# The down projection of a gated MLP as seven products of halves instead of eight

## The chip, the cores and the metric

The kernel runs on one core of a Trainium2 chip. The metric is the device time of one execution in microseconds. TensorE (PE) does the matmuls, VectorE (DVE) and ScalarE (ACT) the elementwise work, GpSimd (POOL) some of it; SyncE (SP) issues nearly all transfers between DRAM and the on-chip memory SBUF. Matmul results land in PSUM, which has eight banks of 128x512 fp32 values.

## The reference, cut to what matters

The layer takes 512 tokens of width 1024. Two attention branches are mixed by gates and added to the residual; then comes the MLP that is changed here, and a last gated addition that uses the same residual:

```python
h = rmsnorm(x, mlp_pre_norm[i])
u = causal_dwconv(h @ w_up[i], conv_w[i], conv_b[i])
u_gate, u_val = jnp.split(u, 2, axis=-1)
ff = (jax.nn.gelu(u_gate, approximate=True) * u_val) @ w_down[i]   # (512 x 2816) @ (2816 x 1024)
x = x + rmsnorm(ff, mlp_post_norm[i])
e = p[i] @ w_ple[i]
x = x + jax.nn.sigmoid(rmsnorm(x, ple_norm[i]) @ w_ple_gate[i]) * e
```

## The kernel before, in words

Every fp32 operand of a matmul is kept as two tiles of a rounded format, `hi` and `lo`, with hi + lo close to the value. `split` (L71) makes them: ACT copies the source to `hi` (L72), DVE subtracts it from the source to get `lo` (L73). `mm3` (L75) then does three matmuls (hi times hi, hi times lo, lo times hi) for every product of a 128x128 stationary tile with a 128x512 moving tile. All matmuls carry line 56, the helper that issues them.

`chunk` (L137) streams weights: SP loads 128x1024 fp32 values (512 KB) into a `raw` tile, and `split` writes a `hi` and a `lo` tile. From the output projection on, these come from rings (`wtile`, L123): 3 raw tiles, 4 hi tiles and 4 lo tiles. A tile of a ring is written again only when the last reader of its earlier use is through.

The up projection runs over 22 pairs j of 128 gate and 128 value columns (L803). A pair needs 48 matmuls of 128x512 (`up_mms`) with `hT`, the normalized tokens, as moving operand, in two PSUM banks; four pairs of banks take turns. `conv_gelu` (L764) follows: for each of the two halves one ACT and two DVE instructions of 128x512 (the convolution), then the gelu on ACT, one multiplication on DVE, and a `split` of the 128x512 result into `ffh[j]` and `ffl[j]`. These 22 tiles live in `xp` (j to 7), `qkp` (j to 15) and `fp` (the last six).

The down projection (`down_pass`, L819) multiplies 512 tokens (four blocks n of 128), 2816 rows (22 tiles k) and 1024 columns (two halves of 512). It goes over the first column half for all four blocks, then over the second for blocks 0 and 1, then again over the second for blocks 2 and 3, 11 weight chunks each time; all eight PSUM banks hold `yd[n][half]`. `post_norm` (L708) normalizes a block, adds it to the residual `xn` and normalizes again; `to_hT` (L725) transposes the result on PE. Blocks 0 and 1 are normalized beside the pass over blocks 2 and 3; blocks 2 and 3 beside the gate matmuls of blocks 0 and 1 (`gate_mms`, L851).

The order of instructions on each engine is not written out by hand. A planner lists them: on each engine, among those that its model of time has ready, it takes the first of the program, or one marked by `hot`. The order is then fixed: each engine and SP's queue works its list from front to back, and an instruction that waits holds all behind it.

Of the kernel before, what the change touches and what calls it, by code (L numbers as in the profile page):

```python
# [8 lines left out]
F32 = mybir.dt.float32  # L9
# [3 lines left out]
ALU = mybir.AluOpType  # L13
# [24 lines left out]
def hybrid_kernel(ctx, tc, T):  # L38
# [634 lines left out]
    for f in (close_ca, close_wk, close_gap, close_sp, close_cqp, close_kvp, close_yp):  # L673
# [128 lines left out]
    g_post, g_next = loadgain(T["mlp_post"]), loadgain(T["ple_norm"])  # L802
    for j in range(2, NPAIR):  # L803
        if j in (8, 16):
            if j == 16:
                fp, close_fp = opened(name="fp", bufs=1, side="right")
            for l, t in ((ffh, "kT"), (ffl, "qT")):
                w = min(8, NPAIR - j)
                f = (qkp if j == 8 else fp).tile([P, w, S], F32R, name="ff" + t, tag=t)
                l.extend(f[:, i, :] for i in range(w))  # L810
# [6 lines left out]
    yd = [banks(n, "yd") for n in range(NB)]  # L817

    def down_pass(half, blocks):  # L819
        for c in range(NPAIR // 2):  # L820
            hi, lo = chunk(T["wd"][half * (NPAIR // 2) + c])
            for kk in range(2):
                k = 2 * c + kk
                w = slice(kk * S, (kk + 1) * S)
                for n in blocks:
                    b = slice(n * P, (n + 1) * P)
                    mm3(yd[n][half], ffh[k][:, b], ffl[k][:, b], hi[:, w], lo[:, w], k == 0, k == NPAIR - 1)

    down_pass(0, range(NB))
    down_pass(1, (0, 1))  # L830
    ts = {n: post_norm(n, yd[n], g_post, g_next) for n in (0, 1)}
    down_pass(1, (2, 3))
    ts[2] = post_norm(2, yd[2], g_post, g_next)
    for n in (0, 1):
        to_hT(n, ts[n])
    ts[3] = post_norm(3, yd[3], g_post, g_next)
    for n in (2, 3):
        to_hT(n, ts[n])


    close_fp()
# [18 lines left out]
    def last_halves(n, half):  # L860
        g = [bank(n, "pg") for _ in range(2)]
        b = slice(n * P, (n + 1) * P)
        for i in range(2):
            u = slice(half * S + i * 256, half * S + (i + 1) * 256)
            for k in range(8):
                hi, lo = cg[k]
                mm3(g[i][:, :256], hT[0][:, k, b], hT[1][:, k, b], hi[:, u], lo[:, u], k == 0, k == 7)
            o = lp.tile([P, S], F32, name="o", tag="o", bufs=4)[:, :256]
            act.activation(o, g[i][:, :256], AF.Sigmoid)
            dve.tensor_tensor(o, o, e[:, n, u], ALU.mult)  # L870
            dve.tensor_tensor(o, o, xn[:, n, u], ALU.add)
# [12 lines left out]

    pg = {(n, half): bank(n, "pg") for n in (0, 1) for half in range(2)}
    gate_mms(pg, (0, 1), (0, 1))
    raw = lp.tile([P, 1024], F32, name="wraw", tag="wraw", bufs=2)
    nc.sync.dma_start(raw, T["pT"].rearrange("p a b -> p (a b)"))
    split(ph.rearrange("p a b -> p (a b)"), pl.rearrange("p a b -> p (a b)"), raw)
    for k in range(2):  # L890
        raw = lp.tile([P, 1024], F32, name="wraw", tag="wraw", bufs=2)
        nc.sync.dma_start(raw, T["wp"][k])
        split(wph[:, k, :], wpl[:, k, :], raw)
    for n in range(NB):
# [15 lines left out]
            gate_mms(g, (n,), (half,))  # L910
            finish(n, half, g[n, half])

    for f in (close_lp, close_ck, close_xnp, close_bcp, close_rawb, close_qkp, close_rawp, close_psp,
              close_hp, close_wb, close_wa, close_xp, close_cpool):
        f()


def layouts(i):
# [16 lines left out]
    wd = np.asarray(i["w_down"])[0].reshape(NPAIR // 2, 2, P, 2, 512).transpose(3, 0, 2, 1, 4)  # L935
    col = lambda v: np.asarray(v).reshape(-1, P).T
    cw = np.asarray(i["conv_w"])[0].reshape(3, 2, NPAIR, P).transpose(0, 3, 2, 1).reshape(3, P, 2 * NPAIR)
    cb = np.asarray(i["conv_b"])[0].reshape(2, NPAIR, P).transpose(2, 1, 0).reshape(P, 2 * NPAIR)
# [21 lines left out]
        "wd": f(wd.reshape(NPAIR, P, 1024)),  # L960
# [45 lines left out]
```

## Time and profile before

| | |
|---|---|
| median of 3 runs | 751.62 us (751.62 to 752.12) |
| the profiled execution | 753.03 us, its span 751.3 us |
| PE busy | 739.1 us, 98% of the span, 3562 matmuls and transposes |
| DVE, ACT, POOL busy | 468.8 us (62%), 349.3 us (46%), 55.5 us (7%) |
| granted TensorE clock, mean | 0.999 of full speed |
| DMA | 81.29 MB, 108 GB/s mean |

The span is the time from the first to the last instruction; what lies around it is the difference to the execution's own time. A matmul's row shows its latency; the next one starts before it ends, so the cost of one is the distance between starts.

### The profile page before, as it was taken

The page shows a single profiled execution, that of the slowest core. Times are in us where ns is not written, and L with a number is a line of the kernel's source. Part 1 is how long each engine was busy: PE and PEld are TensorE (multiplying, and loading weights), DVE is VectorE, ACT ScalarE, POOL GpSimd, SP SyncE. Part 2 cuts the span into 40 slices and gives each one's busy share as a digit, 9 for nine tenths or more (in the row PEclk, how much of TensorE's full clock was granted, in tenths as well). Part 3 has the DMA queues.
Part 4 walks back from the last instruction along what each step waited for, and adds up shares of the span by engine and source line. Part 5 has one row for each costly group of instructions (what it writes and reads, how often), then busy time and mean ns, then how long its engine had stood idle before and what let it go on. Part 6 is the DMA issues. An engine that isn't in the chain of part 4 may idle for free.

```text
span 751.3 us, 9409 instructions
## 1 busy us (share of the span) xinstructions
PE 739.1 (98%) x3562; PEld 615.2 (82%) x3562; DVE 468.8 (62%) x817; ACT 349.3 (46%) x610; POOL 55.5 (7%) x46
## 2 busy tenths in 40 slices
PE   8999999999999999999999999999999999999997
PEld 8988877778888868899888888888888888888886
DVE  6567788986786394757565655666563213486742
ACT  5743577845453243637444444443433114355621
POOL 0104023100000070200000000000000000011200
PEclk9999999999999999999999999999999999999999
DMA  8611221122121327234323232323233233566211
GB/s 300 238 51 64 61 78 49 57 65 76 57 77 65 135 91 282 79 114 117 108 85 111 85 112 85 110 87 95 101 90 106 85 107 127 187 187 215 76 56 57
DMA packets 25582, 81.29 MB, mean 108 GB/s; under 512 B 3296, under 2 KB 4576, under 8 KB 25536
## 3 DMA queue, kind: packets, MB, share of 16 engines
q1 hardware_dynamic: 25536, 80.68, 32.7%
q8 instruction: 28, 0.46, 0.2%
q14 instruction: 18, 0.15, 0.1%
HBM read 78.11 MB, written 2.10 MB: 107 GB/s over the span
## 4 chain that ended last, share of the span: by engine, by line
PE 91%; DVE 7%; issue 1%; DMA 1%; ACT 0%; SPq 0%; DVEq 0%
PE pu L56 29%; PE yd L56 16%; PE psg L56 11%; PE pg L56 6%; PE yo L56 5%; PE puh L56 3%; PE psA L56 3%; PE psba L56 3%; PE psC L56 2%; PE psB L56 2%; PE scm L56 2%; PE pe L56 1%; PE pb L56 1%; PE pvm L56 1%; DVE wlo L73 1%; PE ptm L60 1%
## 5 line engine op out<-in xcount | busy, mean ns | idle before, releaser
L73 DVE TENSOR_TENSOR wlo<-wraw,whi 128x1024 fp32r<-128x1024 f32 (+2 forms) x114 | 140.2, 1231 | 142.6 <-ACT whi L72 139.2
L72 ACT ACTIVATE whi<-wraw 128x1024 fp32r<-128x1024 f32 (+4 forms) x120 | 123.2, 1026 | 159.9 <-PE yd L56 67.1
L56 PE MATMUL pu<-hT,whi 128*128 128x512 f32 x640 | 197.0, 389 | 0.0
L56 PEld LDWEIGHTS pu<-hT,whi 128*128 128x128 f32 x640 | 120.1, 188 | 25.0
L56 PE MATMUL pu<-hT,wlo 128*128 128x512 f32 x320 | 124.5, 389 | 0.0
L56 PEld LDWEIGHTS pu<-hT,wlo 128*128 128x128 f32 x320 | 60.1, 188 | 12.3
L56 PE MATMUL psg<-xh,whi 128*128 128x512 f32 x128 | 51.1, 399 | 1.3 <-DVE ga L422 0.9
L56 PE MATMUL psg<-xl,whi 128*128 128x512 f32 x128 | 50.8, 397 | 0.0
L56 PE MATMUL psg<-xh,wlo 128*128 128x512 f32 x128 | 50.8, 397 | 0.0
L56 PE MATMUL yd<-whi,ffqT 128*128 128x512 f32 x112 | 44.5, 397 | 0.0
L56 PE MATMUL yd<-wlo,ffkT 128*128 128x512 f32 x112 | 44.4, 396 | 0.0
L56 PE MATMUL yd<-whi,ffkT 128*128 128x512 f32 x112 | 44.1, 396 | 0.0
L775 ACT ACTIVATE cv<-cv 128x512 f32<-128x512 f32 x22 | 13.9, 633 | 43.6 <-DVE cv L774 43.6
L715 POOL TENSOR_TENSOR q<-q,mhalf 128x1 f32<-128x1 f32 x8 | 5.3, 657 | 376.8 <-DVE q L714 376.5
L774 DVE SCALAR_TENSOR_TENSOR cv<-pu,pp,cv 128x510 f32<-128x510 f32 x40 | 29.9, 749 | 1.4
L772 ACT ACTIVATE cv<-pu,pp 128x512 f32<-128x512 f32 x40 | 30.5, 761 | 0.0
L56 PEld LDWEIGHTS psg<-xh,whi 128*128 128x128 f32 x128 | 24.1, 188 | 7.0 <-DVE ga L422 1.1
L773 DVE SCALAR_TENSOR_TENSOR cv<-pu,pp,cv 128x511 f32<-128x511 f32 x40 | 29.8, 744 | 0.0
L56 PEld LDWEIGHTS psg<-xl,whi 128*128 128x128 f32 x128 | 24.1, 188 | 4.9 <-issue 0.2
L56 PEld LDWEIGHTS psg<-xh,wlo 128*128 128x128 f32 x128 | 24.1, 188 | 4.8
L72 ACT ACTIVATE ffkT<-cv 128x512 fp32r<-128x512 f32 x14 | 8.9, 633 | 39.1 <-DVE cv L776 39.1
L56 PEld LDWEIGHTS yd<-wlo,ffkT 128*128 128x128 f32 x112 | 21.1, 188 | 5.1
(264 smaller groups left out, 1482.5 us busy)
## 6 DMA issues: line engine op xcount, KB each, us to landing
wraw<-in_wup SPq DMA_DIRECT2D x44, 512.0 KB, 3.4
wraw<-in_wd SPq DMA_DIRECT2D x33, 512.0 KB, 3.4
wraw<-in_wg SPq DMA_DIRECT2D x16, 512.0 KB, 3.4
wraw<-in_wo SPq DMA_DIRECT2D x8, 512.0 KB, 4.2
wraw<-in_wpg SPq DMA_DIRECT2D x8, 512.0 KB, 3.5
xnat<-in_x SPq DMA_DIRECT2D x4, 512.0 KB, 6.4
wraw<-in_wba SPq DMA_DIRECT2D x4, 512.0 KB, 3.4
wraw<-in_wbb SPq DMA_DIRECT2D x4, 512.0 KB, 3.4
```

The lines of the kernel that those rows point to most:

```text
L56: pe.chain(out, nc.tensor.matmul(out, *a, **k))
L60: pe.chain(out, nc.tensor.transpose(out, *a))
L72: act.activation(hi, src, AF.Copy)
L73: dve.tensor_tensor(lo, src, f32(hi), ALU.subtract)
L715: pool.tensor_tensor(r1, v, mhalf[:, :1], ALU.pow)
L772: act.activation(c, u, AF.Identity, scale=w2, bias=cb)
L773: dve.scalar_tensor_tensor(c[:, 1:], u[:, :S - 1], w1, c[:, 1:], ALU.mult, ALU.add)
L774: dve.scalar_tensor_tensor(c[:, 2:], u[:, :S - 2], w0, c[:, 2:], ALU.mult, ALU.add)
L775: act.activation(cs[0], cs[0], AF.Gelu_apprx_tanh)
```

## The change

The result of the down projection is cut into four quarters: token halves 1 and 2 (256 each) by column halves 1 and 2. With A the activations, cut into token halves and two sets of rows (even and odd tiles of 128: pairs c = 0 to 10), and B the weights, cut likewise, the four quarters come from seven products M1 to M7 of sums of A's quarters with sums of B's quarters, each of 256 tokens by 1408 rows by 512 columns.

The sums of A are formed while the up projection runs, once per two pairs j (`ff_sums`): four of the seven operands are split into `FF` in SBUF, three are split and written to DRAM (`d1`, `d2`). The residual `xn` is written to DRAM (`xd`) after the attention part and its SBUF space serves for the sums (`X`); it is loaded again later. The down projection then runs in three stages. Stage 1, over c: M1, M5, M7 and M6 in all eight banks; the weight sums T1, T3 (`t13`) and T2 are formed on DVE. Stage 2, after `drain` has taken the banks' contents: M2 on top of M1, and M3; operands `p1` come back from DRAM, and the odd weight rows are loaded and split a second time. Stage 3: M4, with `p2` from DRAM. Blocks 0 and 1 are normalized beside stage 3, blocks 2 and 3 after it.

```diff
     def post_norm(n, ps, gp, gn):
+        xn = res["xn"]
...
             ts[n] = post_norm(n, yo[n], g_post, g_next)
+            nc.sync.dma_start(xd[n], res["xn"][:, n, :])
...
+    def ff_sums(c):
+        X = Xs.pop(c)
+        dve.tensor_tensor(X[:, 1], X[:, 7], X[:, 6], ALU.add)
+        dve.tensor_tensor(X[:, 3], X[:, 0], X[:, 7], ALU.subtract)
+        dve.tensor_tensor(X[:, 2], X[:, 1], X[:, 0], ALU.subtract)
+        dve.tensor_tensor(X[:, 5], X[:, 4], X[:, 2], ALU.subtract)
+        split(*ff_home(c), X[:, 0:4])
+        h = qp.tile([P, 3, 256], F32R, name="f2h", tag="f2h", bufs=2)
+        l = X[:, 4:7].bitcast(F32R)
+        act.activation(h, X[:, 4:7], AF.Copy)
+        dve.tensor_tensor(l, X[:, 4:7], f32(h), ALU.subtract)
+        for i, v in enumerate((h, l)):
+            nc.sync.dma_start(d1[c][:, i], f32(v[:, 0:2]))
+            nc.sync.dma_start(d2[c][:, i], f32(v[:, 2]))
...
-        dve.tensor_tensor(cs[0], cs[0], cs[1], ALU.mult)
-        split(ffh[j], ffl[j], cs[0])
+        dve.tensor_tensor(Xs[c][:, 4:7:2] if odd else Xs[c][:, 0:8:7], halves(cs[0]), halves(cs[1]), ALU.mult)
+        if odd:
+            ff_sums(c)
...
+    T2t = [hp.tile([P, 8, S], F32, name=f"T2{i}", tag=f"hT{i}") for i in range(2)]
+    T2 = [T2t[c // 8][:, c % 8] for c in range(NC)]
+    T13 = [T2t[1][:, 4 + 2 * i:6 + 2 * i].rearrange("p a t -> p (a t)") for i in range(2)]
+    order4 = ("M1", "M5", "M7", "M6")
...
+    for c in range(NC):
+        r1, r2 = wtile("raw", F32), wtile("raw", F32)
+        nc.sync.dma_start(r1, T["wd"][2 * c])
+        nc.sync.dma_start(r2[:, :S], T["wd"][2 * c + 1][:, B2])
+        t13 = T13[c % 2]
+        h1, l1, h2, l2 = (wtile(k, F32R) for k in ("hi", "lo", "hi", "lo"))
+        split(h1[:, B1], l1[:, B1], r1[:, B1])
+        dve.tensor_tensor(t13[:, B1], r1[:, B2], r1[:, B1], ALU.subtract)
+        dve.tensor_tensor(t13[:, B2], r2[:, :S], r1[:, B2], ALU.subtract)
+        dve.tensor_tensor(T2[c], r2[:, :S], t13[:, B1], ALU.subtract)
+        split(h2, l2, t13)
+        split(h1[:, B2], l1[:, B2], T2[c])
...
+        for m, s in zip(order4, (0, 1, 3, 2)):
+            mms(M[m], [t[:, s] for t in FF[c]], rhs[m], c == 0, c == NC - 1)
+
+    g_post, g_next = loadgain(T["mlp_post"]), loadgain(T["ple_norm"])
+    for n in range(NB):
+        nc.sync.dma_start(xn[:, n, :], xd[n])
...
+    hot(drain)
...
+        nc.sync.dma_start(f32(p1[c]), d1[c])
...
+    for c in range(NC):
+        raw = wtile("raw", F32)
+        nc.sync.dma_start(raw, T["wd"][2 * c + 1])
+        h, l = wtile("hi", F32R), wtile("lo", F32R)
+        split(h, l, raw)
+        dve.tensor_tensor(T4[c], raw[:, B1], T2[c], ALU.subtract)
...
+    for n in range(2):
+        dve.tensor_tensor(V12[n], M3[n], V12[n], ALU.add)
+        ts[n] = post_norm(n, (M["M1"][n], V12[n]), g_post, g_next)
...
+        split(h[:, w], l[:, w], T4[c])
+        mms(M4, [p2[c][:, i] for i in range(2)], (h[:, w], l[:, w]), c == 0, c == NC - 1)
     for n in (0, 1):
+        to_hT(n, ts[n], 1)
+    for n in (2, 3):
+        dve.tensor_tensor(U[n - 2], M4[n - 2], U[n - 2], ALU.add)
+        ts[n] = post_norm(n, (U[n - 2], C22[n - 2]), g_post, g_next)
         to_hT(n, ts[n])
```

In what is left out here, `mms` is `mm3` for two blocks of 128 tokens; `drain` is two ACT copies out of M1 and eight DVE additions of 128x512 that read PSUM; the loop of stage 2 multiplies M2 of c into M1's banks and then M3 of c - 1, six matmuls each; `FF[0..3]` lie in `xp`, `FF[4..7]` in `qkp`, `FF[8..10]` in `fp`; `p1` takes `xp` over, `p2` takes `fp` over, and U, V12, C22 (what `drain` leaves) with T4 lie in `qkp`.

## Rows read from the trace of the kernel before

**Rows 1.** Page, part 1: busy time, share of the span and instructions of each engine.
```profile
PE 739.1 (98%) x3562; PEld 615.2 (82%) x3562; DVE 468.8 (62%) x817; ACT 349.3 (46%) x610; POOL 55.5 (7%) x46
```
**Rows 2.** Page, part 4: shares of the chain that ended last.
```profile
PE 91%; DVE 7%; issue 1%; DMA 1%; ACT 0%; SPq 0%; DVEq 0%
PE pu L56 29%; PE yd L56 16%; PE psg L56 11%; PE pg L56 6%; PE yo L56 5%; PE puh L56 3%; PE psA L56 3%; PE psba L56 3%; PE psC L56 2%; PE psB L56 2%; PE scm L56 2%; PE pe L56 1%; PE pb L56 1%; PE pvm L56 1%; DVE wlo L73 1%; PE ptm L60 1%
```
**Rows 3.** The chain in order of time: start us, us, what.
```profile
565.18 108.72 PE yd L56 x470
673.90 1.75 PE ptr L60 x16
675.65 13.59 PE yd L56 x58
689.23 20.46 PE pg L56 x89
```
**Rows 4.** Waits of PE, longest first: us in total, times, longest us.
```profile
PE psC L56 <- DVE yt L156: 1.2, 1, 1.2
```
**Rows 5.** Timeline of PE in the down projection: start us, us, what.
```profile
584.74 0.39 PE L56 MATMUL yd<-whi,ffh 128*128 128x512 f32 x1
...
586.55 0.39 PE L56 MATMUL yd<-whi,ffl 128*128 128x512 f32 x1
...
587.48 0.40 PE L56 MATMUL yd<-whi,ffkT 128*128 128x512 f32 x1
...
589.82 0.40 PE L56 MATMUL yd<-wlo,ffkT 128*128 128x512 f32 x1
```
**Rows 6.** Stretches: us, PE, PEld, DVE, ACT, POOL busy, PEclk, DMA share, GB/s.
```profile
347.55:565.18 217.63, 217.63 (x962) 180.25 (x961) 135.87 (x165) 96.82 (x126) 0.00 (x0) 1.00 0.31 100
624.20:646.00 21.80, 21.80 (x96) 17.73 (x96) 9.04 (x10) 9.80 (x14) 0.00 (x0) 1.00 0.51 167
656.80:667.00 10.20, 10.20 (x47) 8.41 (x46) 9.32 (x14) 6.90 (x12) 1.65 (x4) 1.00 0.42 120
667.00:689.20 22.20, 22.20 (x105) 18.17 (x104) 14.09 (x15) 10.70 (x15) 1.16 (x1) 1.00 0.63 206
```
**Rows 7.** Groups by form: busy us, mean ns of one, idle before.
```profile
L73 DVE TENSOR_TENSOR wlo<-wraw,whi 128x1024 fp32r<-128x1024 f32 x109 | 137.4, 1262 | 142.6 <-ACT whi L72 139.2 <-issue 2.6 <-PE psg L56 0.8
L72 ACT ACTIVATE whi<-wraw 128x1024 fp32r<-128x1024 f32 x111 | 117.6, 1060 | 152.1 <-PE yd L56 67.1 <-PE pu L56 24.1 <-PE psg L56 23.8
L73 DVE TENSOR_TENSOR ffqT<-cv,ffkT 128x512 fp32r<-128x512 f32 x14 | 9.7, 692 | 9.8 <-ACT ffkT L72 9.8
L73 DVE TENSOR_TENSOR pml<-ptm,pmh 128x384 fp32r<-128x384 f32 x16 | 8.5, 550 | 0.1
```
**Rows 8.** Timeline of DVE beside the tail of the down projection.
```profile
657.84 2.73 DVE L718 SCALAR_TENSOR_TENSOR t<-yd,q,gain 128x512 f32<-128x512 f32 x4
...
661.61 2.35 DVE L719 TENSOR_TENSOR xn<-t,xn 128x1024 f32<-128x1024 f32 x2
...
667.67 2.48 DVE L722 SCALAR_TENSOR_TENSOR t<-xn,q,gain 128x1024 f32<-128x1024 f32 x2
```
**Rows 9.** Timeline of DVE after the last up matmul.
```profile
567.22 0.74 DVE L773 SCALAR_TENSOR_TENSOR cv<-pu,pp,cv 128x511 f32<-128x511 f32 x1
568.00 0.75 DVE L774 SCALAR_TENSOR_TENSOR cv<-pu,pp,cv 128x510 f32<-128x510 f32 x1
568.79 0.69 DVE L776 TENSOR_TENSOR cv<-cv 128x512 f32<-128x512 f32 x1
```
**Rows 10.** DMA issues (KB each, median us to landing), and landing of line 742's four.
```profile
wraw<-in_wd SPq DMA_DIRECT2D x33, 512.0 KB, 3.4
DMA to landing us min/median/max: 4.9/7.1/8.3
```
**Rows 11.** SP's queue: the four loads of line 742 in one row.
```profile
281.68 1.75 SPq L742 DMA_DIRECT2D xn<-in_x  x4
```
**Rows 12.** The stretch of the densest transfers, columns as in rows 6.
```profile
12.00:14.00 2.00, 2.00 (x13) 2.00 (x13) 1.95 (x4) 2.00 (x3) 0.00 (x0) 1.00 1.04 396
```

More of the change, by code (lines that the diff above doesn't have):

```diff
@@ L654, in loadgain @@
     def loadgain(src):
-        t = bcp.tile([P, D], F32, name="gain", tag="gain", bufs=2)
+        t = res["bcp"].tile([P, D], F32, name="gain", tag="gain", bufs=2)
         nc.sync.dma_start(t, src.partition_broadcast(P))
@@ L678, in hybrid_kernel, with open_res, close_res @@
              raw=0, hi=0, lo=0)
-    bcp, close_bcp = opened(name="bcp", bufs=1, side="right")
-    xnp, close_xnp = opened(name="xnp", bufs=1, side="right")
-    xn = xnp.tile([P, NB, D], F32, name="xn")
+    ck, close_ck = opened(name="ck", bufs=1, side="right")
+    fp, close_fp = opened(name="fp", bufs=1, side="right")
+    res = {}
+    def open_res():
+        b, close_b = opened(name="bcp", bufs=1, side="right")
+        x, close_x = opened(name="xnp", bufs=1, side="right")
+        res.update(bcp=b, xn=x.tile([P, NB, D], F32, name="xn"), close=(close_x, close_b))
+    def close_res():
+        for f in res["close"]:
+            f()
+    open_res()
+    dp, close_dp = opened(name="dp", bufs=1, space=bass.MemoryType.DRAM)
     pairs = [[accT, accT], [ptT, ptT], [scT, scT], [scT, pvT]]
@@ L741, in hybrid_kernel @@
     for n in range(NB):
-        nc.sync.dma_start(xn[:, n, :], T["x"][n * P:(n + 1) * P, :])
+        nc.sync.dma_start(res["xn"][:, n, :], T["x"][n * P:(n + 1) * P, :])
+    xd = [dp.tile([P, D], F32, name=f"xd{n}", tag=f"xd{n}") for n in range(NB)]
     g_post, g_next = loadgain(T["attn_post"]), loadgain(T["mlp_pre"])
@@ L752, in hybrid_kernel, with ff_home @@
             to_hT(1, ts[1])
-    ff = [xp.tile([P, 8, S], F32R, name="ff" + t, tag="x" + t) for t in "hl"]
-    ffh, ffl = ([t[:, j, :] for j in range(8)] for t in ff)
+    close_res()
+    qp, close_qp = opened(name="qp", bufs=1, side="right")
+    NC = NPAIR // 2
+    FF = {}
+    Xs = {}
+    d1 = [dp.tile([P, 2, 2, 256], F32, name=f"d1_{c}", tag=f"d1_{c}") for c in range(NC)]
+    d2 = [dp.tile([P, 2, 256], F32, name=f"d2_{c}", tag=f"d2_{c}") for c in range(NC)]
+    def ff_home(c):
+        if c % 4 == 0:
+            p, tags, w = ((xp, ("xh", "xl"), 4), (qkp, ("kT", "qT"), 4), (fp, ("fA", "fB"), 3))[c // 4]
+            t = [p.tile([P, w, 4, 256], F32R, name="ff" + u, tag=u) for u in tags]
+            for i in range(w):
+                FF[c + i] = [v[:, i] for v in t]
+        return FF[c]
+    def ff_sums(c):
[12 more added lines that the diff above has]
+            nc.sync.dma_start(d2[c][:, i], f32(v[:, 2]))
     def up_mms(ps, chs, cols, pcols):
@@ L775, in conv_gelu @@
         act.activation(cs[0], cs[0], AF.Gelu_apprx_tanh)
-        dve.tensor_tensor(cs[0], cs[0], cs[1], ALU.mult)
-        split(ffh[j], ffl[j], cs[0])
+        c, odd = j // 2, j % 2
+        if not odd:
+            Xs[c] = qp.tile([P, 8, 256], F32, name="X", tag="X", bufs=2)
+        halves = lambda t: t.rearrange("p (a t) -> p a t", a=2)
+        dve.tensor_tensor(Xs[c][:, 4:7:2] if odd else Xs[c][:, 0:8:7], halves(cs[0]), halves(cs[1]), ALU.mult)
+        if odd:
+            ff_sums(c)
     chs = {j: [chunk(T["wup"][2 * j + gv]) for gv in range(2)] for j in range(2)}
@@ L801, in hybrid_kernel @@
         conv_gelu(j, [us[j][:, 0, :], us[j][:, 1, :]])
-    g_post, g_next = loadgain(T["mlp_post"]), loadgain(T["ple_norm"])
     for j in range(2, NPAIR):
[L804 to L810, printed above, removed]
         cj = [chunk(T["wup"][2 * j + gv]) for gv in range(2)]
@@ L814, in hybrid_kernel @@
         conv_gelu(j, ps)
-    hT = [hp.tile([P, 8, S], F32R, name=f"h3T{i}", tag=f"hT{i}") for i in range(2)]
[L817 to L833, printed above, removed]
+    close_qp()
+    open_res()
+    xn = res["xn"]
+    vp, close_vp = opened(name="vp", bufs=1, side="right")
+    T2t = [hp.tile([P, 8, S], F32, name=f"T2{i}", tag=f"hT{i}") for i in range(2)]
+    T2 = [T2t[c // 8][:, c % 8] for c in range(NC)]
+    T13 = [T2t[1][:, 4 + 2 * i:6 + 2 * i].rearrange("p a t -> p (a t)") for i in range(2)]
@@ new lines, in hybrid_kernel, with mms @@
+    B1, B2 = slice(0, S), slice(S, 2 * S)
+    order4 = ("M1", "M5", "M7", "M6")
+    M = {m: banks(i, m) for i, m in enumerate(order4)}
+    def mms(ps, lhs, rhs, start, stop):
+        for b in range(2):
+            t = slice(b * P, (b + 1) * P)
+            mm3(ps[b], lhs[0][:, t], lhs[1][:, t], *rhs, start, stop)
+    for c in range(NC):
[10 more added lines that the diff above has]
+        split(h1[:, B2], l1[:, B2], T2[c])
+        rhs = {"M1": (h1[:, B1], l1[:, B1]), "M5": (h2[:, B1], l2[:, B1]),
+               "M7": (h2[:, B2], l2[:, B2]), "M6": (h1[:, B2], l1[:, B2])}
+        for m, s in zip(order4, (0, 1, 3, 2)):
+            mms(M[m], [t[:, s] for t in FF[c]], rhs[m], c == 0, c == NC - 1)
@@ new lines, in hybrid_kernel, with drain @@
+    g_post, g_next = loadgain(T["mlp_post"]), loadgain(T["ple_norm"])
+    for n in range(NB):
+        nc.sync.dma_start(xn[:, n, :], xd[n])
+    T4k = qkp.tile([P, 8, S], F32, name="T4k", tag="kT")
+    T4q = qkp.tile([P, 8, S], F32, name="T4q", tag="qT")
+    T4 = [T4k[:, c] for c in range(8)] + [T4q[:, 0], T4q[:, 1], vp.tile([P, S], F32, name="T4v")]
+    U, V12, C22 = ([T4q[:, 2 + 2 * i + b] for b in range(2)] for i in range(3))
+    def drain():
+        for b in range(2):
+            act.activation(U[b], M["M1"][b], AF.Copy)
+            dve.tensor_tensor(U[b], M["M6"][b], U[b], ALU.add)
+        for b in range(2):
+            dve.tensor_tensor(V12[b], M["M5"][b], U[b], ALU.add)
+            dve.tensor_tensor(U[b], M["M7"][b], U[b], ALU.add)
+            dve.tensor_tensor(C22[b], M["M5"][b], U[b], ALU.add)
@@ new lines, in hybrid_kernel, with m3 @@
+    hot(drain)
+    p1 = []
+    for c in range(NC):
+        if c % 4 == 0:
+            t = xp.tile([P, 4, 2, 2, 256], F32R, name="p1", tag="xl" if c == 4 else "xh")
+        p1.append(t[:, c % 4])
+        nc.sync.dma_start(f32(p1[c]), d1[c])
+    M3 = banks(3, "M3")
+    def m3(c, rhs):
+        mms(M3, [p1[c][:, i, 1] for i in range(2)], rhs, c == 0, c == NC - 1)
+    late = None
+    for c in range(NC):
+        raw = wtile("raw", F32)
[3 more added lines that the diff above has]
+        dve.tensor_tensor(T4[c], raw[:, B1], T2[c], ALU.subtract)
+        for b in range(2):
+            t = slice(b * P, (b + 1) * P)
+            lh, ll = p1[c][:, 0, 0, t], p1[c][:, 1, 0, t]
+            for x, y in ((lh, h), (lh, l), (ll, h)):
+                pe.matmul(M["M1"][b], x, y[:, B1], start=False, stop=c == NC - 1 and x is ll, skip_group_check=True)
+        if late:
+            m3(*late)
+        late = (c, (h[:, B2], l[:, B2]))
@@ new lines, in hybrid_kernel @@
+    m3(*late)
+    hT = [hp.tile([P, 8, S], F32R, name=f"h3T{i}", tag=f"hT{i}") for i in range(2)]
+    ts = {}
+    for n in range(2):
+        dve.tensor_tensor(V12[n], M3[n], V12[n], ALU.add)
+        ts[n] = post_norm(n, (M["M1"][n], V12[n]), g_post, g_next)
+    p2t = [fp.tile([P, 6, 2, 256], F32R, name="p2", tag=t) for t in ("fA", "fB")]
+    p2 = [p2t[c // 6][:, c % 6] for c in range(NC)]
+    for c in range(NC):
+        nc.sync.dma_start(f32(p2[c]), d2[c])
+    M4 = banks(2, "M4")
+    for c in range(NC):
+        if c % 2 == 0:
+            h, l = wtile("hi", F32R), wtile("lo", F32R)
+        w = slice(c % 2 * S, (c % 2 + 1) * S)
+        split(h[:, w], l[:, w], T4[c])
+        mms(M4, [p2[c][:, i] for i in range(2)], (h[:, w], l[:, w]), c == 0, c == NC - 1)
@@ L834, in hybrid_kernel @@
     for n in (0, 1):
+        to_hT(n, ts[n], 1)
+    for n in (2, 3):
+        dve.tensor_tensor(U[n - 2], M4[n - 2], U[n - 2], ALU.add)
+        ts[n] = post_norm(n, (U[n - 2], C22[n - 2]), g_post, g_next)
         to_hT(n, ts[n])
[L836 to L841, printed above, removed]
     cg = [chunk(T["wpg"][k]) for k in range(4)]
-    lp, close_lp = opened(name="lp", bufs=1, side="right")
+    lA = fp.tile([P, 4, S], F32R, name="lA", tag="fA")
@@ L874, in finish @@
     def finish(n, half, pg, parts=1):
-        o = lp.tile([P, S], F32, name="o", tag="o", bufs=4)
+        o = otile()
         q = S // parts
@@ L886, in hybrid_kernel @@
     gate_mms(pg, (0, 1), (0, 1))
-    raw = lp.tile([P, 1024], F32, name="wraw", tag="wraw", bufs=2)
+    raw = wtile("raw", F32)
     nc.sync.dma_start(raw, T["pT"].rearrange("p a b -> p (a b)"))
@@ L890, in hybrid_kernel @@
     for k in range(2):
-        raw = lp.tile([P, 1024], F32, name="wraw", tag="wraw", bufs=2)
+        raw = wtile("raw", F32)
         nc.sync.dma_start(raw, T["wp"][k])
```

24 lines of the change are left out of this document (14 added, 10 removed).

## The prediction

> **What bounds the kernel now.** The busy times come first: PE 98% of the span, DVE 62%, ACT 46% [rows 1]. The chain of waits says whether that is work or waiting: 91% of it is PE, 16% the down projection `yd` [rows 2], and the longest single wait of PE in the whole trace is 1.2 us [rows 4]. So a matmul less is time less, unless PE comes to wait where it doesn't now. In order of time the down projection runs from 565.18 to 689.23 without a break, 1.75 us of transposes included [rows 3].
>
> **Matmuls removed.** Before: 4 blocks x 2 halves x 22 tiles x 3 = 528, in 689.23 - 565.18 - 1.75 = 122.3 us, 0.232 each [rows 3]. After: 7 products x 2 blocks x 11 tiles x 3 = 462. The price of one depends on where the stationary tile lies [rows 5]: from `xp` (ffh) 8 distances take 586.55 - 584.74 = 1.81, 0.226 each; from `qkp` (ffkT) 10 take 2.34, 0.234 each. After, stage 1 has 96 matmuls from `xp` and 168 from the others, stage 2's 132 come from `xp`, stage 3's 66 from `fp`: 228 x 0.226 + 234 x 0.234 = 106.3. That saves 16.0 us. All at 0.234 it would be 14.2, all at 0.226 17.9. I take 15.5, between the two ways of counting (66 x 0.232 = 15.3). The saving is on the path, since PE is.
>
> **Sums of A in the up projection.** DVE durations over length: 692 ns for 512 columns, 550 for 384, 1262 mean (about 1.23 uncontended) for 1024 [rows 7]; on a line through 384 and 512 a 256-wide one takes 0.41, and one of 768 0.96 by the middle of 512 and 1024. Per two pairs j: four sums 1.64, lo's of 1.23 and 0.96, less two of 0.69 that go: +2.45, so +1.2 per pair. DVE has 135.87 us in 20 pairs of 10.88 us, 6.8 each [rows 6]; it comes to 8.0, 74%. ACT: 4.84 per pair [rows 6] plus about 0.3. Cost 0: the 48 matmuls of a pair hide it, and the weight chunks are made tiles ahead. Their cover gone, it would cost 1.2 x 22 = 26, but that needs DVE full, and it is three quarters full. The writes are 0.77 MB per two pairs (8.4 MB) beside 100 GB/s [rows 6], that is +35 GB/s, where 396 have been moved [rows 12]; `xd`'s four lie under the up projection's first matmuls. Each write waits in SP's queue for DVE, and the weight loads behind wait with it, but these are three raw tiles, some 16 us, early. Bounds 0 to 1; I take 0.
>
> **Hand-over from up to down.** Before, the first `yd` matmul starts in its turn [rows 3]. After, stage 1's `t13` and T2 lie in `hT`, which the last up matmul still reads. Back to back a DVE instruction costs about 0.08 less than its row: four 128x512 take 2.73, two 128x1024 2.35 [rows 8], so 0.66 for a convolution step, 0.61 for a plain 512 and 1.14 for a 1024. From the last up matmul: `t13` 1.2, ACT's h2 1.06, l2 1.14, 0.2 of hops: 3.6 us until M5 can start. PE has M1 for c = 0 and c = 1 until then (12 matmuls, 2.7 us; only these, as the hi ring holds two c's). That is the low end, about 1 us. But DVE also has the last pair's two convolution steps and product [rows 9], 1.9, four sums 1.3, and lo's of 1.14 and 0.88, and they are earlier in the program: with all but the lo's first, l2 is done at about 6.0, a wait of 3.3; then two lo's, l1 and c = 1's `t13` and l2, 6.0 us of work against 4.1 of matmuls, 1.9 more. High end 5 to 7. I take 4, nearer the full list, as the planner prefers earlier work.
>
> **Stage 1 after that.** DVE per c: five 512s and a 1024, 4.2 us, against 24 matmuls of 5.4 to 5.6. PE stays the bound: 0.
>
> **Turn to stage 2.** `drain` is hot and takes DVE 8 x 0.61 = 4.9 us, starting 0.7 before the banks are all done. Meanwhile PE has M2 and M3 of c = 0 and 1, 5.4 us, split ahead; lo of c = 2 comes at 4.2 + 1.14 = 5.3. Bounds 0 and 3 (M3 not pulled ahead); I take 0.7. Then 1.75 of DVE per 2.7 of PE.
>
> **Loads.** Stage 1 takes 0.77 MB per c, 2 us at 396 GB/s of 5.5: fine on the mean. But all share SP's queue: six loads of 512 KB (gains, residual) come early in stage 1, eight (`p1`) all at once when c = 3 lets go of `xp`, eleven of 256 KB (`p2`) at stage 2. Issuing costs 0.44 each (four in 1.75) [rows 11], moving 512 KB at 396 GB/s 1.3 [rows 12], so eight put the queue up to 7 us behind, six 5, eleven of half size 2.5. The trace of before has a case: four residual loads in a row land after 4.9 to 8.3 us, against 3.4 for a lone load [rows 10]. A raw tile may land some 2.5 us late before PE sees it: a c's r2 is issued 3.6 after the matmuls of three c's earlier end, and is wanted at 9.5. Bounds 0 (the planner puts weight loads between, each burst is eaten by the lead) and 7 + 5 + 2.5 less three leads, 7 to 9. I take 3.
>
> *The Trainium skill, "DMA: Bandwidth & Descriptors", section "Queues, rings and completion order", says that each engine consumes the descriptors of one queue in ring order, so prefetches issued first delay the weights behind them; the four landing times agree. Were queued loads instead served side by side, the sum would lose nothing on this term, 3 us better.*
>
> **Stage 3 and the norms.** After M3, two `V12` additions, four steps, additions and scalings of 1024: 10 us of DVE, ACT's squares and POOL between. In the trace of before the two norms take from 656.8 to 670.15, 13.3 us, DVE busy 9.32 of 10.20 at first [rows 6, 8]. Now 11 splits of 512 (6.7) lie between them: 16.7 of DVE for 66 matmuls, 15.5 us, some of the splits done earlier. Then the transposes of blocks 0 and 1, with both blocks in one pair of banks, wait for ACT and DVE in turn, about 1. Norms of blocks 2 and 3 lie beside 20.46 us of gate matmuls as before [rows 3]; the late half of the gate weights waits for U and C22 in `qkp`, some 6 us into them, wanted at 11. Bounds 0 and 4.5; I take 1.5.
>
> **Sum.** -15.5 + 4 + 0.7 + 3 + 1.5 = -6.3 us. The profiled execution took 753.03 (span 751.3, 1.7 around it), so 746.7 for one like it; the median of before, 751.62, lies 0.2% lower, which gives 745.3.
>
> **Rivals.**
> - *Slower: the queue.* Eight `p1` loads move in 10.5 us, six gains and residuals in 7.9, eleven `p2` in 7.2. If each stands whole before the weights and exceeds the lead of 2.5, PE waits 8.0 + 5.4 + 4.7 = 18.1 in place of 3. With the other terms: -15.5 + 4 + 0.7 + 18.1 + 1.5 = +8.8, 760; it turns slower from 9.3 us of such waits on. For it: landing of 8.3 [rows 10]. Against it: SP takes 0.44 per issue, so weight loads get in between, and the passes of before ran at 167 to 206 GB/s without a wait [rows 4, 6]. About 754 to 761.
> - *Nothing waits.* The planner puts `t13` and l2 first, loads keep their lead: -15.5 + 1 + 0 + 0 + 1 = -13.5, 738. For it: no PE wait over 1.2 us in a kernel with many such hand-overs [rows 4]. Against it: DVE's list at the hand-over is new.
> - *The clock.* The granted clock reads 1.00, the level of 2.4 GHz, in all stretches shown [rows 6, 12]. If the waits of 3 to 5 us at the hand-over or behind loads make it fall to 1.2 GHz, the matmuls after them run at half rate, and each five of 0.23 cost 1.1 us more. At three places of, say, 15 matmuls that is 10 us: -6.3 + 10 = +3.7, 755; at one place 749. No row shows a fall, hence a small chance.
> - *The Trainium skill, "TensorE: Matmul & The Clock Gate", section on the clock gate, says that an idle PE falls back to 1.2 GHz; that is the rule of this last rival.*
>
> **How the numbers follow.** Forecast 0.56 (739 to 750, all faster), nothing waits 0.12 (736 to 739), the queue 0.21, the clock 0.11. Bounds of the forecast's own terms: -17.9 + 1 to -14.2 + 7 + 3 + 9 + 4.5. The range 737 to 757 leaves out a little of the no-wait case and the upper half of the queue's. 0.2% (1.5 us, what a measurement tells apart) as no change: 0.06 of the queue's share and 0.03 of the clock's, 0.09. Faster 0.56 + 0.12 + 0.02 = 0.70; slower 0.21.
>
> **What would show it.** 462 matmuls in place of 528, at 0.226 to 0.234. At the hand-over PE waits for a DVE lo of L73 (h2's) 3 to 5 us; none there: nothing waits. ACT or DVE waiting for `wraw<-in_wd` landings over 6 us in stages 1 and 2: the queue. PEclk below 1.00: the clock. PE waiting before the transposes: stage 3. The forecast is wrong if PE's waits after the up projection exceed 14 us or stay below 5, or if the up projection's 217.6 us grow.

## The result, and the profile after

The changed kernel is slower: 757.37 us median of 7 runs (754.14 to 758.93) against 751.82 (751.62 to 752.28), ratio 1.0068 [1.0049, 1.0087]. The forecast was 745.3, its range ended at 757. The profiled run took 756.0 us, with a span of 754.2: 2.9 us more than the span before, where the medians differ by 5.6, as it is one of the three faster of the seven runs, which show a mean granted clock of 0.991 or 0.992, the four slower ones 0.986 to 0.989.

The page of the kernel after: busy times, the granted clock in 40 slices, the shares of the chain.

```profile
PE 730.6 (97%) x3496; PEld 606.4 (80%) x3496; DVE 533.3 (71%) x939; ACT 362.8 (48%) x634; POOL 49.8 (7%) x46
...
PEclk9999999999999999999999999999999979999999
...
PE 77%; DVE 11%; DMA 9%; issue 2%; ACT 1%; SPq 0%; ACTq 0%; DVEq 0%
```

The 66 instructions are gone (3562 to 3496) and PE's busy time fell by 8.5 us [rows 1]; yet PE's share of the chain went from 91% to 77% [rows 2], and DMA, at 1% before, has 9%. The waits of PE, longest first (us in total, times, longest us):

```profile
PE M L56 <- ACT whi L72: 10.1, 4, 5.4
PE ptr L60 <- DVE h3T L748: 1.5, 1, 1.5
PE pg L56 <- ACT h3T L747: 1.4, 1, 1.4
```

Before, the longest was 1.2 [rows 4]. ACT's split is named since it ends last; what it waits for stands in the chain in time order (start us, us, what):

```profile
593.80 10.87 DMA wraw<-in_wd
604.69 0.69 DVE T L883
605.38 0.61 DVE T L884
606.03 9.51 DMA wraw<-in_wd
...
653.47 8.37 DMA wraw<-in_wd
...
716.54 11.25 PE pe L56 x48
```

Three weight loads took 8.4 to 10.9 us. The third is a whole chunk of 512 KB, which lands after 3.4 alone [rows 10]; the first two are half chunks of 256 KB (line 878), whose landings are

```profile
DMA to landing us min/median/max: 2.7/3.5/10.9
```

SP's queue at the first two says what they stood behind:

```profile
588.86 0.40 SPq L877 DMA_DIRECT2D wraw<-in_wd  x1
589.35 0.38 SPq L915 DMA_DIRECT2D p<-d  x1
589.82 0.38 SPq L656 DMA_DIRECT2D gain<-in_mlp_post  x1
590.25 0.73 SPq L656 DMA_DIRECT2D gain<-in_ple_norm  x1
591.08 2.31 SPq L894 DMA_DIRECT2D xn<-xd  x4
593.80 0.33 SPq L878 DMA_DIRECT2D wraw<-in_wd  x1
595.06 0.33 SPq L877 DMA_DIRECT2D wraw<-in_wd  x1
596.34 8.67 SPq L915 DMA_DIRECT2D p<-d  x7
606.03 0.33 SPq L878 DMA_DIRECT2D wraw<-in_wd  x1
```

Fourteen side loads of 512 KB in 15.7 us, with two weight loads among them. The seven loads of `p1` in one row took 1.24 us each to go (8.67 / 7), not the 0.44 of [rows 11]. What SP waits for from 588 to 608 us (us in total, times, longest us) says why:

```profile
SPq L915 <- DMA xn<-xd: 5.0, 4, 1.6
SPq L877 <- DMA p<-d: 1.7, 2, 0.9
SPq L878 <- DVE T L884: 1.3, 2, 1.0
SPq L915 <- DMA gain<-in_mlp_post: 0.9, 1, 0.9
SPq L915 <- DMA gain<-in_ple_norm: 0.9, 1, 0.9
```

In this row SP sends each load only when the one issued eight before it has landed: the first gain, issued at 589.82, landed 6.50 us later, at 596.32, and the load of 596.34 is the eighth behind it. Most of the landings come 1.3 us apart, which is 512 KB at the 406 GB/s of the next table. The stretches there (us, PE, PEld, DVE, ACT, POOL busy, PEclk, DMA share, GB/s):

```profile
590.00:600.00 10.00, 10.00 (x44) 8.03 (x43) 6.01 (x9) 2.38 (x4) 0.00 (x0) 1.00 0.99 360
600.00:610.00 10.00, 4.60 (x14) 3.35 (x13) 4.32 (x6) 2.10 (x3) 0.00 (x0) 0.72 1.02 406
610.00:620.00 10.00, 7.18 (x25) 5.33 (x25) 4.10 (x6) 2.10 (x3) 0.00 (x0) 0.84 0.72 275
```

The DMA engines are full for 20 us, and PE stands still for 5.40 and 2.82 of the 20 from 600 us on; then its clock is down as well. PE's timeline after these two waits (in brackets the idle time before):

```profile
606.61 3.78 PE L56 MATMUL M<-whi,ffkT 128*128 128x512 f32 x8 [5.40 <-ACT whi L72]
610.18 0.63 PE L56 MATMUL M<-wlo,ffkT 128*128 128x512 f32 x1
610.61 0.63 PE L56 MATMUL M<-whi,ffqT 128*128 128x512 f32 x1
611.04 0.50 PE L56 MATMUL M<-wlo,ffkT 128*128 128x512 f32 x1
611.38 0.39 PE L56 MATMUL M<-whi,ffqT 128*128 128x512 f32 x1
...
617.39 2.35 PE L56 MATMUL M<-whi,ffkT 128*128 128x512 f32 x6 [2.82 <-ACT whi L72]
```

Starts lie 0.43 us apart (610.18, 610.61, 611.04), the level of 1.2 GHz, and 0.23 from 611.38 on (the next at 611.61), that of 2.4. From 606.61 to 611.38 there are 11 matmuls in 4.77 us; at 0.234 they would take 2.57, so 2.2 are lost. After the second wait 1.6 are lost in the same way (11 from 617.39 to 621.60).

### The profile page after: what moved, and what is told of

It is laid out like the page before. It is cut to its first block, busy times and chain, and to the rows that moved or that the text cites. A ratio compares the mean times of both kernels' runs of the same rounds, so it can differ in the third digit from the quotient of the medians.

```text
span 754.2 us, 9531 instructions
## 1 busy us (share of the span) xinstructions
PE 730.6 (97%) x3496; PEld 606.4 (80%) x3496; DVE 533.3 (71%) x939; ACT 362.8 (48%) x634; POOL 49.8 (7%) x46
## 2 busy tenths in 40 slices
DMA packets 36239, 99.90 MB, mean 132 GB/s; under 512 B 4481, under 2 KB 8577, under 8 KB 36193
## 4 chain that ended last, share of the span: by engine, by line
PE 77%; DVE 11%; DMA 9%; issue 2%; ACT 1%; SPq 0%; ACTq 0%; DVEq 0%
PE pu L56 29%; PE psg L56 11%; DMA wraw<-in_wd 7%; PE yo L56 6%; PE pg L56 6%; DVE wlo L73 3%; PE puh L56 3%; PE M L56 3%; PE psA L56 3%; PE psba L56 3%; PE psC L56 2%; PE psB L56 2%; PE pe L56 1%; PE scm L56 1%; PE pb L56 1%
## 5 line engine op out<-in xcount | busy, mean ns | idle before, releaser
L72 ACT ACTIVATE whi<-wraw 128x1024 fp32r<-128x1024 f32 (+4 forms) x109 | 106.5, 979 | 162.9 <-PE pu L56 75.2
L73 DVE TENSOR_TENSOR wlo<-wraw,whi 128x1024 fp32r<-128x1024 f32 (+2 forms) x103 | 119.4, 1161 | 65.7 <-ACT whi L72 62.0
L56 PEld LDWEIGHTS pu<-hT,wlo 128*128 128x128 f32 x320 | 60.1, 188 | 12.3
L56 PE MATMUL M<-whi,p 128*128 128x512 f32 x132 | 41.4, 393 | 1.0 <-ACT whi L72 1.0
L72 ACT ACTIVATE whi<-T 128x1024 fp32r<-128x1024 f32 (+1 forms) x22 | 17.8, 838 | 38.3 <-DVE T L883 38.2
L56 PEld LDWEIGHTS M<-whi,p 128*128 128x128 f32 x132 | 24.7, 188 | 6.8 <-ACT whi L72 1.4
L56 PE MATMUL M<-wlo,p 128*128 128x512 f32 x66 | 26.0, 394 | 0.1
L670 POOL TENSOR_TENSOR gx<-gx,ga 128x512 f32<-128x512 f32 x8 | 14.8, 1869 | 133.3 <-DVE gx L669 133.3
```

The source lines that it names most:

```text
L56: pe.chain(out, nc.tensor.matmul(out, *a, **k))
L72: act.activation(hi, src, AF.Copy)
L73: dve.tensor_tensor(lo, src, f32(hi), ALU.subtract)
L670: pool.tensor_tensor(ta, ta, ga[:, m, :], ALU.add)
```

## The experiments

In the diffs, `after(a, b)` only fixes the order in SP's queue: a stands behind b. W1 and W2 are the lists of the odd-row weight loads of stages 1 and 2. The first four ran beside the kernel before at 752.24 us, the next four at 752.23, the last two at 752.33.

**1. `p1` spread over stage 1.**

```diff
-        nc.sync.dma_start(f32(p1[c]), d1[c])
+        ins = nc.sync.dma_start(f32(p1[c]), d1[c])
+        if c < 8:
+            after(ins, W1[6 + c // 2])
```

> The changed kernel with one change: the eight p1 loads that come in one row in stage 1 are issued two at a time, each pair behind the weight loads of c = 6 to 9; same bytes, same arithmetic. Theory Q (weight loads stand behind prefetches in SP's queue): the second wait of stage 1 (2.8 us and about 2.0 us of matmuls at 1.2 GHz behind it) goes, the first (5.4 us, behind one p1, two gains and four residual loads) becomes one load shorter, about 4: some 6 us less than the changed kernel, 751. Rival B (the sum of the transfers is too much for the 16 engines, the order does not matter): 757 as it is. Rival D (DVE is late with the splits): 757 as it is.

Measured: 750.85 us (748.74 to 751.87), ratio to before 0.9983 [0.9975, 0.9992]. The order of one kind of loads is worth 6.5 us and brings the change level with the kernel before. One wait of 4.33 at 604.21 stays, as expected: the six gains and residuals alone are row enough for it.

**2. Gains and residual moved to stage 2.**

```diff
-    g_post, g_next = loadgain(T["mlp_post"]), loadgain(T["ple_norm"])
-    for n in range(NB):
-        nc.sync.dma_start(xn[:, n, :], xd[n])
...
+        if c in (3, 6):
...
+            after(nc.sync.dma_start(g, T["mlp_post" if c == 3 else "ple_norm"].partition_broadcast(P)), W2[c])
...
+        if c in (4, 5):
+            after(nc.sync.dma_start(xn[:, c - 4, :], xd[c - 4]), W2[c])
+        if c in (9, 10):
+            after(nc.sync.dma_start(xn[:, c - 7, :], xd[c - 7]), W2[c])
```

> The changed kernel with the other change: the two gains and the four residual loads are issued one by one in stage 2, behind its weight loads; p1 as it was. Theory Q: six of the seven loads of the first row go from stage 1, the eight p1 loads still stand in one row: one wait of about 5 us with its half clock stays, the second goes: 751, with up to 1 us given back in stage 2. Rival B: 757. Rival D: 757.

Measured: 756.23 us (755.60 to 756.95), 1.0053 [1.0041, 1.0065]; the expectation of 751 missed. The first wait is still 4.96 us: `p1`'s eight loads, seven of them in a row, are row enough too. And the six moved loads now meet `p2` in stage 2, where PE waits 1.21, 1.22 and 1.74.

**3. Both.** The edits of 1 and 2 together.

> Both changes of the two runs before together. Theory Q: stage 1 has no wait of PE above 1 us and the granted clock stays at 1.00 there: 5.4 + 2.8 us of waits and about 4 us of half clock go, 757.4 - 12.2 = 745, faster than the kernel before by 0.9%. Rival B: the bytes are the same, 757. Rival D: 757, with the waits still behind DVE's splits.

Measured: 747.55 us (746.44 to 749.07), 0.9941 [0.9929, 0.9952]. The two edits are worth 9.8 together, 6.5 and 1.1 alone: they are not two costs but one row, which delays the weights until it is broken up altogether. That is 2.5 us short of the 745 expected. Stage 1 has no wait but the 0.89 at its start. In stage 2 three waits of 0.18, 1.25 and 1.75 remain, where `p2` and the rest of `p1` stand in a row, and the clock falls once more. (The 4.1 us that the expectation of run 5 gives to stage 2 are these 3.2 and the 0.89.)

**4. The side loads in another queue.** Gains, residual, `p1` and `p2` are issued by GpSimd instead of SP; the line of `p1` stands for all.

```diff
-        nc.sync.dma_start(f32(p1[c]), d1[c])
+        nc.gpsimd.dma_start(f32(p1[c]), d1[c])
```

> The changed kernel with gains, residual, p1 and p2 loads issued by GpSimd instead of SP, in the order that the planner gives them; weights alone in SP's queue; bytes the same. Theory Q in its strict form (it is the place in SP's queue): weights no longer stand behind the prefetches, they share the engines with them; a weight load lands in about twice 3.4 us at worst, PE waits 0 to 3 us in stage 1: 745 to 750. Rival B (sum of the transfers): waits stay as they are, 757.

Measured: 751.20 us (748.97 to 754.17), 0.9983 [0.9972, 0.9994], between the two theories and nearer the first. DMA issues from 560 us on (KB each, median us to landing):

```profile
wraw<-in_wd SPq DMA_DIRECT2D x20, 512.0 KB, 5.2
p<-d POOLq DMA_DIRECT2D x11, 512.0 KB, 9.0
```

With the weights alone in SP's queue the longest wait on a weight tile falls from 5.4 us to 1.4, and all of them together from 10.1 to 5.4. They don't vanish: the other queue keeps the engines at 407 GB/s, and a weight load still takes 5.2 us. *The Trainium skill, "DMA: Bandwidth & Descriptors", section "Issuing engines are not separate DMA queues", says that loads issued by several engines run on the same 16 DMA engines and interleave, and that this saves only the time of issuing. The sharing shows in these rows; the saving was more than that here, 6.2 us, as a load in a queue of its own doesn't stand behind the whole row.*

**5. Every side load behind a weight load.** The first eight of `p1` as in 1; gains, residual, `p2` and the rest of `p1` one or two at a time behind weight loads, the last six in a row behind the last of them.

```diff
+    LOADS = {0: "g1", 1: "x0", 2: "x1", 3: "x2", 4: "p20 p21", 5: "p22 p23", 6: "p18", 7: "p19", 8: "p110",
+             9: "p24 p25", 10: "p26 p27 p28 p29 p210 x3"}
...
+            after(ins, W2[c])
```

> The changed kernel with every side load of the down projection (the two gains, the four tiles of the residual, p1 and p2) put in SP's queue one or two at a time behind a weight load of stage 1 or 2, where before seven to twelve of them stood in a row. Theory A (a row of side loads in the queue of the weights is what makes TensorE wait, because the weight buffers hold little more than one pair of chunks): stage 2's waits, 4.1 us in all in the run with p1, gains and residual paced, and the half clock behind them (1 to 2 us) go, the time is 742 to 744 us, and no wait of TensorE on a weight tile is over 1 us. Theory B (in stages 1 and 2 the bytes themselves are too many for the DMA engines, in whatever order): the waits only move, the time stays at 746 to 749 us.

Measured: 743.67 us (742.33 to 744.79), 0.9885 [0.9870, 0.9900], as theory A said: 13.7 us less than the changed kernel, with the same 99.90 MB and the same instructions but for their order. SP's queue in the stretch that was the worst, and the stretch itself:

```profile
591.68 0.33 SPq L883 DMA_DIRECT2D wraw<-in_wd  x1
592.06 0.42 SPq L920 DMA_DIRECT2D p<-d  x1
592.59 0.37 SPq L882 DMA_DIRECT2D wraw<-in_wd  x1
593.01 0.42 SPq L920 DMA_DIRECT2D p<-d  x1
596.25 0.33 SPq L882 DMA_DIRECT2D wraw<-in_wd  x1
596.86 0.33 SPq L883 DMA_DIRECT2D wraw<-in_wd  x1
```
```profile
600.00:610.00 10.00, 10.00 (x44) 8.02 (x44) 7.61 (x11) 3.68 (x5) 0.00 (x0) 1.00 0.91 324
610.00:620.00 10.00, 10.00 (x45) 8.03 (x44) 7.84 (x13) 4.00 (x6) 0.00 (x0) 1.00 0.99 354
```

PE has no gap at 324 and 354 GB/s and a DMA share of 0.91 to 0.99. From 590 to 620 us the DMA engines move nearly as much as in the changed kernel (318 GB/s, 347 there). So it was not the bytes: DMA engines this full didn't hurt here, with at most two side loads between two weight loads.

**6. The same, and the tail.** Block 1's transposes use the banks of M3 instead of sharing two with block 0.

```diff
-        to_hT(n, ts[n], 1)
+        to_hT(n, ts[n], (1, 3)[n])
```

> As the kernel with every side load paced, and besides the transposes of the second token block use the PSUM banks of the product that ended last instead of sharing two banks with the first block's. Theory A (the tail's waits of 1.4 and 1.5 us are for the copies that empty these two banks): 1.5 to 3 us less than that kernel, 740 to 742 us. Theory B (the second block's transposes wait for its sums, norm or gain on VectorE): no change, 742 to 744 us.

Measured: 741.00 us (740.43 to 743.60), 0.9859 [0.9843, 0.9875]. This version beats both kernels: 1.41% under the one before. PE's timeline at the tail:

```profile
672.50 1.03 PE L60 MATMUL ptr<-ident,t 128*128 128x128 f32 x8
674.95 0.50 PE L56 MATMUL pg<-whi,h3T 128*128 128x512 f32 x1 [1.42 <-ACT h3T L747]
...
677.69 0.96 PE L56 MATMUL pg<-whi,h3T 128*128 128x512 f32 x3 [0.67 <-DVE h3T L748]
```

The wait of 1.5 before the second transposes is gone; 0.67 stands in its place, so the waits are worth 0.9. Most of the rest of the 2.7 us against run 5 lies with the clock: run 5's profile has a granted clock of 0.85 from 670 to 680 us, behind waits of 1.42 and 1.54, and here it is 1.00; from the first transpose to `pe` it took 30.8 us there and takes 28.4 here.

**7. A row put into the kernel before.** 16 stores of 512 KB to an unused tile, in front of one weight load; nothing else moves.

```diff
+        for i, d in enumerate(dd):
+            ins = nc.sync.dma_start(d, f32(hT[i % 2][:, 2 * (i // 2 % 4):2 * (i // 2 % 4) + 2, :]))
+            tc.add_manual_dep(ins.ins, W["load"].ins.name, order, reason="queue order")
```

> The kernel before, whole, plus 16 stores of 512 KB to an unused DRAM tile, put in SP's queue in a row in front of one weight load of the down projection's second column half; nothing else moves. 16 such transfers at 1.3 us each hold the queue for about 21 us. Theory A (a row in the weights' queue becomes a wait of TensorE only as far as it is longer than the weight buffers hold work, 11 to 14 us here): a wait of 7 to 10 us and 1 to 2 us of half clock, 760 to 764 us against 752. Theory B (the queue does not hold the weight load back: the 16 DMA engines take both side by side): no wait over 2 us, 752 to 754 us.

Measured: 759.23 us (759.06 to 760.21), 1.0095 [1.0082, 1.0109]; 7.0 us slower, just below theory A's 760, with a wait of 5.0 for its 7 to 10. Two rows of SP's queue, and PE's timeline after its wait:

```profile
617.18 18.85 SPq L824 DMA_DIRECT2D dd<-hT  x16
636.14 12.52 SPq L141 DMA_DIRECT2D wraw<-in_wd  x6
```
```profile
644.39 1.17 PE L56 MATMUL yd<-whi,ffkT 128*128 128x512 f32 x2 [5.00 <-ACT whi L72]
...
646.24 0.63 PE L56 MATMUL yd<-whi,ffqT 128*128 128x512 f32 x1
646.67 0.63 PE L56 MATMUL yd<-wlo,ffkT 128*128 128x512 f32 x1
```

Each part of the changed kernel's loss is made here in the kernel before: 1.18 us per issue in a row, a wait, starts 0.43 apart. (It is done with stores, and here the issues themselves last up to 1.3 us; in the changed kernel they last 0.33, and SP waits for landings between them.) The weight loads come 5.6 us apart, the last at 616.81, so the next was due at about 622.4; it went at 636.14 and took 7.04 us to land instead of 3.4: 13.7 + 3.6 = 17.3 late, of which PE felt 5.0. The rings of the kernel before thus covered some 12.3 us.

**8. 66 matmuls less, and nothing else.**

```diff
+                    if half == 0 and n > 0:
+                        pe.matmul(yd[n][0], ffh[k][:, b], hi[:, w], start=k == 0, stop=False)
+                        pe.matmul(yd[n][0], ffh[k][:, b], lo[:, w], start=False, stop=k == NPAIR - 1)
+                        continue
```

> The kernel before with 66 of its 528 matmuls of the down projection left out (the third product of the split for three of the four token blocks in the first column half; the output is that much less exact) and nothing put in. It measures the first term of the sum by itself. If a left-out matmul is worth its 0.232 us of TensorE, as forecast: 15.3 us less, 736 to 737 us. If the weight loads or ScalarE's split of them set the pace in part: 738 to 745 us.

Measured: 737.63 us (736.42 to 737.97), 0.9803 [0.9789, 0.9816]: 14.6 us less (13.8 to 15.9 by the interval), 0.221 per matmul. The forecast's 15.5 lies in that interval: the first term of the sum was right.

**9. Half the row.** As 7, with 8 stores.

> The kernel before plus 8 stores of 512 KB in a row in front of the same weight load as the 16 of the earlier run. With 16 the row held the queue 19.0 us, the load behind it landed 3.6 us later than a lone one, and PE waited 5.0 us: the rings covered 17.6 us. Theory A (a row costs TensorE only what it exceeds the lead): 8 stores delay the load by some 10 to 11 us, all covered; no wait of PE over 0.5 us on a weight tile, 752 to 753 us. Theory B (each transfer put ahead costs its share, half of the 7.0 us that 16 cost): 755 to 756 us.

Measured: 751.67 us (750.96 to 753.94), 0.9995 [0.9986, 1.0003]. SP's queue:

```profile
616.03 0.33 SPq L141 DMA_DIRECT2D wraw<-in_wd  x1
616.41 8.60 SPq L824 DMA_DIRECT2D dd<-hT  x8
625.11 13.45 SPq L141 DMA_DIRECT2D wraw<-in_wd  x6
```

PE is busy for all of 610 to 630 us, and no wait of PE stands in the trace behind that in the down projection. Eight stores cost nothing, sixteen 7 us: a row has no price of its own, only what it exceeds the lead. (The 17.6 us in the expectation counts from the front of the row, not from when the load was due; 12.3 is the lead.)

**10. The tail alone,** in the changed kernel with its queue as it is; the edit of 6.

> The changed kernel with only the second block's transposes moved to the PSUM banks of the product that ended last; its queue stays as it is. Theory A (the tail's waits stand at the end of the path, whatever waits before them): as much less as in the kernel with paced loads, 1 to 3 us, 754.5 to 756.5 us. Theory B (the gain there was the clock level after two waits close together, which this kernel's profile does not show at that place): 757 us, no change.

Measured: 754.20 us (752.88 to 756.07), 1.0022 [1.0013, 1.0031] to before, against 1.0068 [1.0049, 1.0087] for the changed kernel. Theory A: it gains whatever waits before it. In the profiled runs the tail is 0.9 us shorter (28.4 for 29.35 from the first transpose to `pe`). That the other 2 us or so are the clock, in runs without a profile, is likely after run 5 but not shown.

## Why the prediction was wrong

Its terms against the two profiled executions:

| term | forecast, us | measured, us |
|---|---|---|
| 66 matmuls less | -15.5 | -14.4 |
| sums in the up projection | 0 | 0 |
| hand-over | +4 | +0.9 |
| stage 1's work, turn to stage 2 | +0.7 | 0 |
| loads | +3 | +13.5 |
| stage 3 and the norms | +1.5 | +3.7 |
| sum | -6.3 | +3.7 |

The span itself grew by 2.9; of the difference 0.35 is the earlier start of the down projection (564.83 for 565.18) and 0.5 the part from `pe` on. The table explains these 2.9 us; what makes up the rest of the 5.6 between the medians is not shown.

**Matmuls.** In run 6, where nothing is late, the products take from 563.55 to 672.50 with 1.1 us of waits in it: 107.9, 0.2335 each, near the upper of the two distances of [rows 5]. Before it was 122.3 [rows 3], so 14.4 are saved; run 8 has 14.6.

**Up projection.** 217.4 us after, 217.63 before [rows 6], with 155 us of DVE work in it instead of 135.9. The cover that the prediction named was there.

**Hand-over.** Four times too dear. The prediction let DVE do the last pair's convolution first, "as the planner prefers earlier work". The planner put the four weight subtractions first (564.80 to 567.22 on DVE), then one convolution step and l2 (567.88). PE waited 0.89, the low end of its own bounds: the order of DVE's list was not the program's order where several instructions were ready. (The pieces that the prediction gives for l2, 1.9 + 1.3 + 3.6, make 6.8, not its 6.0; that decided nothing.)

**Loads: the step that failed.** The prediction put 3 us on it. PE's waits there are 5.40 + 2.82 + 1.03 = 9.25. The products take 122.36 us in the changed kernel (564.83 to 687.19), less its waits of 10.14, 112.2; at full clock 107.9. So 4.3 more went to the half clock (3.8 by the spacing above), 13.5 in all. That decides the sign: with the loads at 3 the measured terms would make -6.8. Of three assumptions of that step two gave way, and the third did not help:

- *"six loads of 512 KB (gains, residual) come early in stage 1, eight (`p1`) all at once when c = 3 lets go of `xp`"*. They came at once. The residual's space is X's, and the last instruction of `ff_sums`, which the prediction had some 8 us behind the up projection, came at 586.5 us on DVE, 22 us into stage 1; `xp` came free at the same time (first load of `p1` at 589.35). Two bursts, each to be eaten by a lead, became one row of 15.7 us.
- *"Issuing costs 0.44 each", so "the planner puts weight loads between".* That is the price with idle engines. With full ones it was 1.24 (after), 1.18 and 1.08 (runs 7 and 9): the queue itself stands still. Two weight loads of 16 transfers got in between. By run 5 (593.80 here is 591.68 there, where the same loads go 0.93 to 1.38 us earlier up to then) the first went only about 1 us late; it was its landing, behind seven side loads in flight, that took 8 too long.
- *"A raw tile may land some 2.5 us late."* This was not far off. By run 5 the load at 606.03 (596.86 there) was due at about 598. It went 8 late: the row in front of it ended at 605.0, and its raw tile came free at 606.0, when DVE had read the late load before it. It landed some 6.7 late (9.51 for 2.8), 14.7 in all. PE stood or crawled for 5.40 + 2.2 + 2.82 = 10.4 of it, so about 4 were covered, against 12.3 before (run 7). Eight transfers in a row cost nothing before (run 9); the eight loads of `p1` alone, seven of them in a row, cost a wait of 4.96 after (run 2). The likely reason is that a c takes two tiles of each ring for its 24 matmuls, where a chunk of the first pass of before took one, and the rings were not deepened. No run here has deeper rings, so this reason is argued, not shown.

The rival that was called the queue had the mechanism. That 9.25 us of waits were measured, where it gives 9.3 as the point from which the change turns slower, is luck: by the measured terms without the half clock the point is 9.8, and it is the half clock that carries the change past it. Its price of 18.1 was too high because one row has one lead to eat, and `p2` cost 1.03 instead of 4.7. The rival of the clock was right as well, but as the other's tail: two falls of some 2 us each instead of three of 3.3. By the measured terms neither alone makes the kernel slower; together they do. Of the signs that the prediction named, the landings over 6 us and PEclk below 1.00 came true; its own limit of 14 us of PE's waits did not, as they were 13.1 (0.89 + 9.25 + 1.42 + 1.55) and it left out what the clock takes behind a wait. *The rule that the prediction cited from the Trainium skill ("DMA: Bandwidth & Descriptors", "Queues, rings and completion order": descriptors of one queue are consumed in ring order) should have weighed more: by it the load behind seven waits for all seven, and 10.87 us, against 2.7 at best for such a half chunk, agrees.*

**Stage 3 and the norms.** From the last product to `pe` it took 29.35 us (687.19 to 716.54); before, 23.85 (689.23 to 713.08) and 1.75 of transposes that lay earlier [rows 3]: 3.7 more, 3.0 of them the waits of 1.42 and 1.55. The forecast had about 1 for these.

The measured column with loads at 0.2 and the tail at 2.8, as in run 6, makes -10.5: run 6 measured -11.2 by medians.

## What to carry to other kernels

Before side loads are put on the queue that feeds the critical engine, ask which of them become free to go at the same moment, price the whole row at 1.1 to 1.25 us per 512 KB, and hold it against the lead of the rings, measured and not counted: three raw tiles at two per 5.6 us would be 8.4 us here, and about 4 were covered. A change that uses two tiles where there was one needs a fresh look at it. Then place each side load by hand behind a weight load; here that order alone was 13.7 us, almost as much as the 66 matmuls.

## What the hardware showed

- TensorE fell to the 1.2 GHz level behind waits of 2.82 and 5.40 us in the changed kernel, 4.33 in run 1, 4.96 in run 2, 5.00 in run 7, 3.60 and 5.09 in run 10, each time for 7 to 14 matmuls, which took 1.4 to 2.7 us more than at full clock; the longest wait was not the dearest. After single waits of 0.89 and 1.03 it did not fall. Short waits close together made it fall in some cases: after 1.25 and 1.75 in run 3, after 1.42 and 1.54 with four matmuls between them in run 5, but not after 1.42 and 1.55 in the changed kernel.
- In a row of 512 KB transfers SP's issue goes at the pace of the transfers, 1.08 to 1.24 us each, not at its own 0.33 to 0.44. In the changed kernel each load of the row went within 0.1 us of the landing of the one issued eight before it.
- Loads of 512 KB kept the 16 engines at 400 to 410 GB/s for 10 us and more, above the 396 of [rows 12].
